# A decoder step's FFN on one core: the second token half's operands made early and kept in DRAM, products paired in PSUM banks

## The chip, the core and the metric

The kernel runs on one core of a Trainium2 chip. The time is device microseconds (us) of one launch; the figure to compare is the median of 3 runs. [...]

## The reference

One layer of a conditioned hybrid decoder over 1024 prompt tokens and 8 x 4 sample tokens (1056 in all), width 1024: a mixer (three kinds of recurrence), then the FFN that the change touches, then a last norm.

```
x = x + gate_m * concat(y_A, y_B, y_C) @ w_out
h = rms_norm(x, norm_ffn_w) * (1 + scale_f) + shift_f
g, u = split(h @ w_ffn_in)            # 1024 -> 2 x 2816
x = x + gate_f * ((silu(g) * u) @ w_ffn_out)
y = rms_norm(x, final_norm_w)
```

## The kernel before

The program is recorded, not written in order: every operation goes through `Plan.record`, and `Plan.order` lists them engine by engine with a cost table, the lowest key first among those that are ready (the key is the place of recording, less what `priority(n)` gives); tiles come from pools of numbered buffers (`tile(..., bufs)`), and `give` hands buffers of one tag to another once the first tag is done. So all rows of a profile bear one line, L632 (L639 after the change), and work is told apart by the tiles' names.

Values are kept as two fp32r parts, high and low, and one product is three matmuls (`dmm`: hi x hi, hi x lo, lo x hi). Splitting a tile is a cast on ACT (the high part) and a subtraction on DVE or POOL (the low part): `wh`, `wl` for weights, `act` pairs for the FFN's input, `raw` pairs for its inner values.

The tokens are cut into four pieces of 264 (`HW`), and the FFN runs twice (`g` = 0, 1), each time over two pieces, with all weights loaded again. In one `g`:

- `ffn_input` makes 7 operands (blocks) of 4 x 264 columns from x1: the normed pieces b11, b21, b12, b22 and their differences, as one two-by-two block product with seven products instead of eight needs them. Each block has a high and a low `act` tile; 14 of the 16 `act` tiles are in use.
- for each of 22 `f`, `ffn_up` loads four weight tiles of 256 KB (a11, a12: gate; a21, a22: up), forms s1 to s4 from them, splits seven weights, runs seven products of 12 matmuls each (84), adds them up on DVE in `sl` tiles, applies Silu on ACT, multiplies, and splits the result into `raw` pairs.
- after every second `f`, `down` loads four tiles of w_ffn_out and runs 16 groups of 6 matmuls (96), whose results DVE adds to x1 (`kp` tiles, `gated_half`). The last piece holds the 32 sample tokens, whose gates differ (`gated_seq`, a small `ga` tile).

A period below is this round of two `f` and one `down`: 168 + 96 = 264 matmuls. Weights are loaded into `wr` (4 buffers, plus the given ones: one of `tq`, one of `s0`, two of `int`), and split into four `wh`/`wl` pairs. At the end of `g` = 0, `ffn_input(..., 1)` uses again the `act` tiles that `g` = 0 read; at `g` = 1, `f` = 2, `final(x1, 0)` normalizes and writes the first 384 tokens in one go.

Of the kernel before, what the change touches and what calls it, by code (L numbers as in the profile page):

```python
# [13 lines left out]
F32 = mybir.dt.float32  # L14
# [52 lines left out]
ENGW = "ppvpvpvpvvv"  # L67
LEVELS = (1, 2, 4, 8, 16, 32)
# [171 lines left out]
class Plan:  # L240
# [17 lines left out]
    def tile(self, pool, shape, dt, tag, bufs=1, like=None):  # L258
# [8 lines left out]
        return View(t, ap.bitcast(dt) if ap.dtype != dt else ap, ())  # L267

# [380 lines left out]
class Step:  # L649
# [866 lines left out]
    def dmm(self, o, terms, first=True, last=True):  # L1516

        n = len(terms)
        for i, ((wh, wl), (xh, xl)) in enumerate(terms):
            self.nc.tensor.matmul(o, wh, xh, start=first and i == 0, stop=False)  # L1520
            self.nc.tensor.matmul(o, wh, xl, start=False, stop=False)
            self.nc.tensor.matmul(o, wl, xh, start=False, stop=last and i == n - 1)
# [171 lines left out]
    def ffn_input(self, x1, rs, sc, g):  # L1694
# [5 lines left out]

        def h(k, hf, i):
            t = self.raw()[:, 0:HW]
            x = x1[k]
            for si, o, d, n in self.half(hf, T):
                en(XR[4 * g + i]).tensor_tensor(t[:, d:d + n], x[si][:, o:o + n], rs[hf][:, d:d + n], op=ALU.mult)
            n = min(HW, TP - HW * hf)
            sh = self.mod[:, 3 * KT + k]
            if TSE[4 * g + i] == "s":
                nc.scalar.activation(t[:, 0:n], t[:, 0:n], AF.Identity, scale=sc[:, k, 0:1], bias=sh[:, 0:1])
            else:  # L1710
                nc.vector.tensor_scalar(t[:, 0:n], t[:, 0:n], sc[:, k, 0:1], sh[:, 0:1], op0=ALU.mult, op1=ALU.add)
            if n < HW:
                tv = t[:, n:HW].rearrange("p (q i) -> p q i", i=TQ)
                nc.vector.tensor_tensor(tv, tv, sc[:, k, 1:9].unsqueeze(2).broadcast_to([P, NQ, TQ]), op=ALU.mult)
                nc.vector.tensor_tensor(tv, tv, sh[:, 1:9].unsqueeze(2).broadcast_to([P, NQ, TQ]), op=ALU.add)
            return t

        def put(i, j, t):
            self.split(blk[i][0][:, j], blk[i][1][:, j], t, en(LOE[7 * g + i]))

        en = lambda c: nc.gpsimd if c == "p" else nc.vector
        b11 = []
        b21 = []
        for j in range(KH):
            b11.append(h(j, 2 * g, 0))
            put(0, j, b11[j])
# [471 lines left out]
```

## Time and profile before

| what | value |
|---|---|
| three runs | 1806.72, 1808.59, 1818.21 us; median 1808.59 |
| the profiled execution | 1816.74 us, its span 1814.9 us |
| busy | PE 94%, DVE 78%, ACT 53%, POOL 52% |
| mean granted TensorE clock | 0.958 |
| chain that ended last, by engine | PE 76%, DVE 10%, ACT 7% |

PE's busy share says that it nearly always has a matmul in flight, not that it works at its peak: a matmul that waits in the pipe, or runs at the lower clock level, counts as busy. So the argument goes by matmuls in a stretch of time, stage by stage. The mixer ends at about 920 us of the span; the output projection, the two FFN halves and the last norm fill the rest.

### The profile page before, as it was taken

Reading aid. Unit: us, or ns where it says so; the run is one execution under the profiler, and the core shown is the slowest. Engines: PE = TensorE matmul, PEld = TensorE weight load, DVE = VectorE, ACT = ScalarE, POOL = GpSimd, SP = SyncE. Lnnn points to the kernel's source line nnn. Section 1 sums busy time; section 2 is a strip of 40 time slices with the busy share of each in tenths; the row PEclk is TensorE's granted clock in tenths of the full one; section 3 lists DMA queues with packets and bytes.
Section 4 is the critical chain, followed back from the end, with each engine's and each line's share of the span. In section 5 each row is a group of like instructions: output and inputs, shape, how many; then the busy total and the mean of one; then the engine's idle time right before and its main releaser. Section 6 shows DMA issues by size and latency. Waiting matters only on the chain.

```text
span 1814.9 us, 43501 instructions
## 1 busy us (share of the span) xinstructions
PE 1710.4 (94%) x16278; PEld 1492.6 (82%) x16278; DVE 1407.0 (78%) x3426; ACT 964.9 (53%) x2406; POOL 946.8 (52%) x1068
## 2 busy tenths in 40 slices
PE   5999999999999999999899999999997889999995
PEld 2787776777788877777699999999996889999995
DVE  6664575777766667667758889899999989999997
ACT  5654555746666556768736555434445534434434
POOL 5552332533455535565527665666667546646645
PEclk9999898999999988999799999999997999999997
DMA  8313113123342211113342232332321232323321
GB/s 286 110 50 108 35 52 105 46 60 109 74 132 51 68 32 40 35 48 110 107 136 81 73 100 81 102 102 94 110 83 60 76 105 94 107 80 94 105 82 67
DMA packets 152923, 158.28 MB, mean 87 GB/s; under 512 B 67620, under 2 KB 94472, under 8 KB 152712
## 3 DMA queue, kind: packets, MB, share of 16 engines
q1 hardware_dynamic: 152136, 154.92, 28.3%
q8 instruction: 128, 2.10, 0.5%
q14 instruction: 83, 0.68, 0.1%
q10 hardware_dynamic: 576, 0.59, 0.1%
HBM read 142.55 MB, written 12.89 MB: 86 GB/s over the span
## 4 chain that ended last, share of the span: by engine, by line
PE 76%; DVE 10%; ACT 7%; issue 3%; DMA 2%; POOL 1%; SPq 0%; DVEq 0%; ACTq 0%; POOLq 0%
PE psd L632 29%; PE psc L632 15%; PE psg L632 14%; PE psm L632 10%; PE psi L632 8%; DVE kp L632 3%; DVE sl L632 2%; ACT sl L632 2%; ACT wh L632 2%; DVE act L632 1%; DVE wl L632 1%; DMA wr<-in_w_ada_dram 1%; ACT s L632 1%; DVE raw L632 1%; ACT ts L632 1%
## 5 line engine op out<-in xcount | busy, mean ns | idle before, releaser
L632 PE MATMUL psd<-act,wh 128*128 128x384 f32 (+3 forms) x2144 | 543.7, 331 | 18.7 <-ACT act L632 11.8
L632 POOL TENSOR_TENSOR wl<-wr,wh 128x512 fp32r<-128x512 f32 (+1 forms) x215 | 302.7, 1411 | 265.2 <-ACT wh L632 240.7
L632 PEld LDWEIGHTS psd<-act,wh 128*128 128x128 f32 x2144 | 372.1, 194 | 44.8 <-ACT act L632 15.2
L632 PE MATMUL psd<-act,wl 128*128 128x384 f32 (+3 forms) x1048 | 344.0, 328 | 2.6 <-POOL wl L632 1.6
L632 ACT CAST wh<-wr 128x512 fp32r<-128x512 f32 (+1 forms) x277 | 169.9, 618 | 194.3 <-PE psd L632 45.7
L632 ACT ACTIVATE sl<-sl 128x384 f32<-128x384 f32 (+5 forms) x400 | 187.7, 483 | 59.9 <-DVE sl L632 44.4
L632 PEld LDWEIGHTS psd<-act,wl 128*128 128x128 f32 x1048 | 203.3, 194 | 14.3 <-issue 3.7
L632 PE MATMUL psc<-act,wh 128*128 128x264 f32 (+2 forms) x776 | 157.4, 291 | 6.0 <-ACT act L632 3.9
L632 PE MATMUL psg<-act,wh 128*128 128x264 f32 (+1 forms) x784 | 157.8, 291 | 2.2 <-DVE act L632 1.1
L632 POOL TENSOR_TENSOR sl<-sl,sl 128x384 fp32r<-128x384 f32 (+5 forms) x84 | 83.9, 1000 | 102.5 <-ACT sl L632 39.9
L632 PEld LDWEIGHTS psc<-act,wh 128*128 128x128 f32 x776 | 123.2, 190 | 9.4 <-ACT act L632 5.1
L632 PEld LDWEIGHTS psg<-act,wh 128*128 128x128 f32 x784 | 124.9, 191 | 6.7 <-issue 2.0
L632 PE MATMUL psg<-act,wl 128*128 128x264 f32 (+1 forms) x392 | 113.9, 291 | 2.8 <-POOL wl L632 2.2
L632 PE MATMUL psc<-act,wl 128*128 128x264 f32 (+2 forms) x388 | 112.7, 290 | 1.5 <-POOL wl L632 1.1
L632 ACT COPY ts<-psg 64x128 f32<-64x128 f32 (+1 forms) x272 | 75.9, 279 | 63.8 <-PE psc L632 44.7
L632 POOL TENSOR_TENSOR wl<-int,wh 128x512 fp32r<-128x512 f32 (+1 forms) x61 | 85.7, 1407 | 41.5 <-ACT wh L632 38.3
L632 DVE TENSOR_TENSOR sl<-sl,sl 128x264 f32<-128x264 f32 (+2 forms) x136 | 93.9, 699 | 8.3 <-ACT sl L632 7.4
L632 POOL TENSOR_TENSOR wl<-tq,wh 128x512 fp32r<-128x512 f32 x42 | 59.2, 1410 | 61.5 <-ACT wh L632 61.1
L632 DVE TENSOR_TENSOR xb<-xb,qb 96x30 f32<-96x30 f32 (+3 forms) x270 | 85.0, 315 | 3.1
L632 ACT CAST wh<-int 128x512 fp32r<-128x512 f32 (+1 forms) x108 | 66.5, 615 | 37.0 <-PE psc L632 6.5
L632 ACT CAST raw<-sl 128x264 fp32r<-128x264 f32 x88 | 36.2, 411 | 91.1 <-DVE sl L632 20.5
L632 DVE TENSOR_TENSOR qb<-nb,xb 96x30 f32<-96x30 f32 (+3 forms) x270 | 76.3, 282 | 10.2 <-DMA xb<-in_masks_dram 6.3
(332 smaller groups left out, 4683.6 us busy)
## 6 DMA issues: line engine op xcount, KB each, us to landing
wr<-in_w_fi_dram SPq DMA_DIRECT2D x94, 256.0 KB
wr<-in_w_ada_dram SPq DMA_DIRECT2D x80, 256.0 KB
wr<-in_w_in_dram SPq DMA_DIRECT2D x62, 256.0 KB
wr<-in_w_fo_dram SPq DMA_DIRECT2D x49, 256.0 KB
int<-in_w_fi_dram SPq DMA_DIRECT2D x34, 256.0 KB
tq<-in_w_fi_dram SPq DMA_DIRECT2D x29, 256.0 KB
kp<-in_xT_dram SPq DMA_DIRECT2D x32, 192.0 KB
s<-in_w_fi_dram SPq DMA_DIRECT2D x19, 256.0 KB
```

Source lines behind the costliest of these rows:

```text
L632: getattr(getattr(nc, o.eng), o.fn)(*[real(a) for a in o.args], **{k: real(a) for k, a in o.kw.items()})
```

## The change

- The operands of `g` = 1 are made during `g` = 0: `ffn_stage` is a generator, started after `f` = 4, which makes one block column after another in new `hb` tiles (given by `int`, `ix` and `lora`), splits it into the two `act` tiles that were free, and writes it to DRAM (`xop`), 56 writes of 132 KB. It is advanced twice after each `f`. At `g` = 1, `ffn_back` fetches the seven blocks in 14 transfers of 528 KB.
- `int` buffers no longer go to `wr`.
- In `ffn_up` the products come in another order (x0, x3, x5, x2, x1, x4, x6); the first and the fifth, and the third and the seventh, are summed in one bank by PE; Silu, the products of gate and up, and the difference are written back in place in PSUM. DVE does five additions per `f`, not seven. Weight splits and sums are recorded with `priority(WPR)`, WPR = 100.
- `gated_seq` works in place in the bank, without `ga`.
- `final(x1, 0)` is advanced by one step per `f`.

```diff
@@ Step
+    def ffn_parts(self, x1, rs, sc, g, j, b11, b21, put, alloc):
...
+        b12 = h(j, 2 * g + 1, 2)
+        b22 = h(KH + j, 2 * g + 1, 3)
+        t1 = (self.hb if g else self.sl)()[:, 0:HW]
+        en(TAD[4 * g + 0]).tensor_tensor(t1, b12, b11, op=ALU.subtract)
+        t2 = (self.hb if g else self.sl)()[:, 0:HW]
+        en(TAD[4 * g + 1]).tensor_tensor(t2, b22, t1, op=ALU.subtract)
+        put(2, j, t2)
+        yield
...
+    def ffn_stage(self, x1, rs, sc):
...
+        self.xop = [nc.tile("dr", [P, 2, KH, HW], F32, f"xop{i}") for i in range(7)]
+        stg = [self.act()[:, 0:KH * HW].rearrange("p (k n) -> p k n", n=HW) for i in (0, 1)]
...
+        def put(i, j, t):
+            c = next(turn)
+            hi, lo = (st[:, c] for st in stg)
+            self.split(hi, lo, t, en(LOE[7 + i]))
+            for v, a in enumerate((hi, lo)):
+                nc.sync.dma_start(self.xop[i][:, v, j], a.bitcast(F32))
...
+    def ffn_back(self):
+        blk = [None] * 7
+        for i in (0, 3, 5, 2, 1, 4, 6):
+            blk[i] = [self.act()[:, 0:KH * HW] for v in (0, 1)]
+            for v in (0, 1):
+                self.nc.sync.dma_start(blk[i][v].bitcast(F32), self.xop[i][:, v].rearrange("p k n -> p (k n)"))
...
@@ ffn_up
-        nc.scalar.copy(p1, prod(w1, x[0]))
-        acc(ga, p1, prod(w2, x[1]))
-        nc.scalar.activation(ga, ga, AF.Silu)
-        u2 = p1
-        acc(u2, p1, prod(w6, x[2]))
-        acc(u3, u2, prod(ws(s3), x[3]))
-        c21 = self.sl()[:, 0:HW]
-        acc(c21, u3, prod(ws(a22), x[4]), ALU.subtract)
-        p5 = prod(ws(s1), x[5])
-        acc(u3, u3, p5)
-        acc(u4, u2, p5)
+        pa = prod(w1, x[0])
+        nc.scalar.copy(u2, pa)
+        pc = prod(w3, x[3])
+        pb = prod(w4, x[5])
+        acc(u2, u2, prod(ws(s2), x[2]))
+        acc(u3, u2, pc)
+        nc.scalar.activation(ga, prod(ws(a12), x[1], pa), AF.Silu)
+        pe = prod(ws(a22), x[4])
+        acc(pe, u3, pe, ALU.subtract)
+        acc(u3, u3, pb)
         s4 = a12
         add(s4, a12, s2)
-        acc(gb, u4, prod(ws(s4), x[6]))
-        nc.scalar.activation(gb, gb, AF.Silu)
+        prod(ws(s4), x[6], pb)
+        acc(pb, u2, pb)
+        nc.scalar.activation(pb, pb, AF.Silu)
         out = []
-        for a, b in ((ga, c21), (gb, u3)):
+        for a, b in ((pe, ga), (pb, u3)):
             nc.vector.tensor_tensor(a, a, b, op=ALU.mult)
@@ gated_seq
-        t = self.small(TS, tag="ga", bufs=2)
+        t = ps[:, d:d + TS]
@@ tile_hybrid_step_kernel
+    nc.make("sb", "hb")
+    for tag, to, n in (("tq", "wr", KH * P), ("s0", "wr", KH * P), ("int", "hb", HW), ("ix", "hb", HW), ("lora", "hb", HW)):
...
         if g:
-            x = st.ffn_input(x1, rs, sc2, 1)
+            x = st.ffn_back()
...
+            if g == 0 and f == 4:
+                late = st.ffn_stage(x1, rs, sc2)
             if g == 1 and f == 2:
-                for _ in st.final(x1, 0, o_y):
-                    pass
+                late = st.final(x1, 0, o_y)
+            with nc.priority(-LATER):
+                next(late, None)
+                if not g:
+                    next(late, None)
```

How the instructions stand, at three places. All engines' rows are the same as before up to the output projection.

DVE, before, at the end of the first half: `raw` and `sl` are the normed pieces and their differences, `act` the operand parts, `wl` a weight's low part.

```order
L632 TENSOR_TENSOR raw_907_33547<-raw_907_33547,mod_89 128x32
L632 TENSOR_TENSOR sl_909_33585<-raw_906_33534,raw_887_32883 128x264
L632 TENSOR_TENSOR wl_107<-int_112,wh_102 128x512
L632 TENSOR_TENSOR sl_910_33598<-raw_907_33547,sl_909_33585 128x264
L632 TENSOR_TENSOR act_128<-sl_909_33585,act_127 128x264
L632 TENSOR_TENSOR act_122<-sl_910_33598,act_121 128x264
L632 TENSOR_TENSOR act_124<-raw_906_33534,act_123 128x264
L632 TENSOR_TENSOR act_126<-raw_901_33455,act_125 128x264
L632 TENSOR_TENSOR act_130<-raw_907_33547,act_129 128x264
```

The five subtractions into `act` stand in one run there, four such runs one behind another. DVE, after, inside the first half (`int` and `lora` are `hb` buffers, `act_133` and `act_134` the staging pair):

```order
L639 TENSOR_TENSOR psc_117<-sl_714_26961,psc_117 128x264
L639 TENSOR_TENSOR sl_714_26961<-sl_714_26961,psd_151 128x264
L639 TENSOR_TENSOR psc_117<-psc_117,sl_713_26916 128x264
L639 TENSOR_TENSOR act_133<-int_112,act_134 128x264
L639 TENSOR_TENSOR act_133<-int_113,act_134 128x264
L639 TENSOR_TENSOR wl_106<-wr_96,wh_103 128x512
L639 TENSOR_TENSOR psd_151<-sl_712_26779,psd_151 128x264
L639 TENSOR_TENSOR raw_717_27096<-psc_117,raw_716_27035 128x264
L639 TENSOR_TENSOR act_133<-lora_94,act_134 128x264
L639 TENSOR_TENSOR psd_151<-psd_151,sl_714_26961 128x264
L639 TENSOR_TENSOR wl_105<-wr_97,wh_100 128x512
L639 TENSOR_TENSOR raw_719_27160<-psd_151,raw_718_27149 128x264
```

The operands' subtractions now stand between the first half's own rows, and those own rows have a bank as output (`psc`, `psd`).

SP, before, at the end of the first half: four rows of its last w_ffn_out weights and the four of the second half's first `f` (`tq`, `int` and `s_0` are weight buffers):

```order
L632 DMA int_112<-in_w_fo_dram 128x512
L632 DMA int_113<-in_w_fo_dram 128x512
L632 DMA wr_97<-in_w_fo_dram 128x512
L632 DMA tq_198<-in_w_fo_dram 128x512
L632 DMA wr_98<-in_w_fi_dram 128x512
L632 DMA wr_99<-in_w_fi_dram 128x512
L632 DMA s_0_195<-in_w_fi_dram 128x512
L632 DMA wr_96<-in_w_fi_dram 128x512
```

Nothing stands between them. SP, after, at the same place: `xop` are the operands in DRAM, of which block 0 was fetched earlier into the staging pair; the four w_fi rows are a11, a12, a21, a22 of the second half's first `f`.

```order
L639 DMA tq_198<-in_w_fo_dram 128x512
L639 DMA act_121<-xop_0_209 128x1056
L639 DMA act_122<-xop_0_209 128x1056
L639 DMA wr_98<-in_w_fi_dram 128x512
L639 DMA act_123<-xop_0_212 128x1056
L639 DMA act_124<-xop_0_212 128x1056
L639 DMA wr_97<-in_w_fi_dram 128x512
L639 DMA act_127<-xop_0_214 128x1056
L639 DMA act_128<-xop_0_214 128x1056
L639 DMA wr_99<-in_w_fi_dram 128x512
L639 DMA s_0_195<-in_w_fi_dram 128x512
```

Of that `f`, a11 and a12 now stand behind four and five fetched blocks, and a21 and a22 behind all six.

PE, before, in the first `f` of the second half, third and later products:

```order
L632 MATMUL psd_151<-act_120,wh_102 128x264
L632 MATMUL psd_151<-act_119,wl_107 128x264
L632 MATMUL psd_150<-act_127,wh_102 128x264
L632 MATMUL psc_117<-act_123,wh_103 128x264
L632 MATMUL psg_152<-act_121,wh_101 128x264
L632 MATMUL psd_150<-act_128,wh_102 128x264
L632 MATMUL psd_150<-act_127,wl_107 128x264
```

Three products' rows alternate. PE, after, at the same place (`act_121` is block 1 with a12's parts, `act_123` block 4 with a22's, `act_125` block 5 with s1's):

```order
L639 MATMUL psm_111<-act_121,wh_102 128x264
L639 MATMUL psm_111<-act_122,wh_102 128x264
L639 MATMUL psm_111<-act_121,wl_105 128x264
L639 MATMUL psi_172<-act_123,wh_102 128x264
L639 MATMUL psi_172<-act_124,wh_102 128x264
L639 MATMUL psi_172<-act_123,wl_105 128x264
L639 MATMUL psg_153<-act_125,wh_100 128x264
L639 MATMUL psg_153<-act_126,wh_100 128x264
L639 MATMUL psi_172<-act_123,wh_102 128x264
```

After the products of a11 and a12, the third product in line is that of a22, then those of s1 and s3.

## Rows read from the trace of the kernel before

**Rows 1.** Windows by stage: busy us (instructions) of each engine, clock, DMA.

```profile
core 0: us, PE busy (x) PEld busy (x) DVE busy (x) ACT busy (x) POOL busy (x), PEclk, DMA share, GB/s
1117.27:1345.41 228.14, 227.85 (x1850) 225.86 (x1849) 205.99 (x407) 98.79 (x196) 139.88 (x99) 1.00 0.31 98
1494.62:1767.44 272.82, 266.82 (x2114) 259.73 (x2113) 248.95 (x594) 113.56 (x224) 156.40 (x112) 1.00 0.30 94
1366.96:1494.62 127.66, 106.39 (x712) 97.44 (x711) 116.00 (x252) 60.86 (x127) 74.79 (x65) 0.85 0.24 77
...
1767.44:1814.90 47.46, 29.00 (x190) 25.53 (x188) 34.50 (x80) 21.03 (x42) 24.02 (x21) 0.81 0.18 64
961.20:1117.27 156.07, 151.95 (x1186) 146.94 (x1187) 138.75 (x269) 90.00 (x203) 104.90 (x94) 1.00 0.27 85
```

**Rows 2.** Windows of 10 us around the start of the second half, same columns.

```profile
1360.00:1370.00 10.00, 10.00 (x84) 10.00 (x83) 8.34 (x16) 5.89 (x13) 8.53 (x8) 1.00 0.58 182
...
1380.00:1390.00 10.00, 6.25 (x20) 4.12 (x18) 8.53 (x15) 8.95 (x20) 10.00 (x14) 0.67 0.09 27
1390.00:1400.00 10.00, 5.65 (x17) 4.24 (x18) 9.49 (x21) 6.10 (x14) 7.84 (x10) 0.50 0.16 52
...
1460.00:1470.00 10.00, 7.12 (x34) 6.41 (x35) 6.46 (x20) 4.08 (x6) 4.69 (x3) 0.66 0.37 118
```

**Rows 3.** PE's waits from 1366.96 to 1494.62: total us, times, longest us.

```profile
PE psd L632 <- ACT act L632: 6.3, 5, 2.5
```

**Rows 4.** PE's timeline in the second half: start us, us, [idle before, releaser].

```profile
1599.87 0.40 PE L632 MATMUL psg<-act,wh 128*128 128x264 f32 x2
1600.57 0.39 PE L632 MATMUL psg<-act,wl 128*128 128x264 f32 x1 [0.29 <-POOL wl L632]
```

**Rows 5.** DVE's groups, 1494.62 to 1767.44: count, busy us, mean ns.

```profile
L632 DVE TENSOR_TENSOR wl<-int,wh 128x512 fp32r<-128x512 f32 x22 | 28.5, 1294 | 0.4
L632 DVE TENSOR_TENSOR sl<-sl,sl 128x264 f32<-128x264 f32 x32 | 25.8, 824 | 0.0
L632 DVE TENSOR_TENSOR kp<-kp,ga 128x32 f32<-128x32 f32 x64 | 20.6, 323 | 0.0
L632 DVE TENSOR_TENSOR raw<-sl,raw 128x264 fp32r<-128x264 f32 x32 | 19.2, 600 | 6.7 <-ACT raw L632 6.5
...
L632 DVE TENSOR_TENSOR sl<-sl,psc 128x264 f32<-128x264 f32 x28 | 11.9, 425 | 6.0 <-PE psc L632 5.7
...
L632 DVE TENSOR_TENSOR wr<-int,wr 128x512 f32<-128x512 f32 x9 | 6.1, 679 | 0.0
...
L632 DVE TENSOR_TENSOR ga<-psd,mod 128x32 f32<-128x32 f32 x32 | 5.7, 177 | 0.0
```

**Rows 6.** DVE's groups, 1117.27 to 1345.41, same columns.

```profile
L632 DVE TENSOR_TENSOR raw<-sl,raw 128x264 fp32r<-128x264 f32 x28 | 21.5, 769 | 2.7 <-ACT raw L632 2.7
L632 DVE TENSOR_TENSOR sl<-sl,sl 128x264 f32<-128x264 f32 x29 | 21.5, 740 | 4.2 <-ACT sl L632 3.4
```

**Rows 7.** DVE's groups, 1366.96 to 1470, same columns.

```profile
L632 DVE TENSOR_TENSOR act<-raw,act 128x264 fp32r<-128x264 f32 x18 | 10.4, 593 | 4.1 <-ACT act L632 4.0
...
L632 DVE TENSOR_TENSOR act<-sl,act 128x264 fp32r<-128x264 f32 x8 | 5.4, 684 | 0.5 <-ACT act L632 0.5
...
L632 DVE TENSOR_TENSOR raw<-raw,mod 128x32 f32<-128x32 f32 x8 | 3.2, 405 | 0.0
```

**Rows 8.** Windows: five us near the program's start, columns as Rows 1.

```profile
10.00:15.00 5.00, 2.61 (x6) 1.50 (x7) 1.02 (x5) 2.54 (x9) 0.97 (x1) 1.00 1.05 375
```

**Rows 9.** Timelines of SP, DVE and ACT in the first half: issues and first readings of two loads.

```profile
1196.49 0.33 SPq L632 DMA_DIRECT2D wr<-in_w_fi_dram  x1
...
1200.44 0.68 DVE L632 TENSOR_TENSOR wr<-tq,wr 128x512 f32<-128x512 f32 x1
...
1207.66 0.33 SPq L632 DMA_DIRECT2D wr<-in_w_fo_dram  x1
...
1215.21 0.62 ACT L632 CAST wh<-wr 128x512 fp32r<-128x512 f32 x1 [1.17 <-PE psi L632]
```

More of the change, by code (lines that the diff above doesn't have):

```diff
@@ L67 @@
 ENGW = "ppvpvpvpvvv"
+WPR = 100
+LATER = 0
 LEVELS = (1, 2, 4, 8, 16, 32)
@@ L267, in tile, with make @@
         return View(t, ap.bitcast(dt) if ap.dtype != dt else ap, ())
+    def make(self, pool, tag):
+        self.phys[tag] = []
+        self.space[tag] = pool
     def give(self, tag, to, cut):
@@ L1514, in wr, with dmm @@
         return self.nc.tile("sb", [P, KH, P], F32, "wr", 4)
-    def dmm(self, o, terms, first=True, last=True):
+    def dmm(self, o, terms, first=True, last=True, on=False):
         n = len(terms)
+        kw = {"skip_group_check": True} if on else {}
         for i, ((wh, wl), (xh, xl)) in enumerate(terms):
-            self.nc.tensor.matmul(o, wh, xh, start=first and i == 0, stop=False)
-            self.nc.tensor.matmul(o, wh, xl, start=False, stop=False)
-            self.nc.tensor.matmul(o, wl, xh, start=False, stop=last and i == n - 1)
+            self.nc.tensor.matmul(o, wh, xh, start=first and i == 0, stop=False, **kw)
+            self.nc.tensor.matmul(o, wh, xl, start=False, stop=False, **kw)
+            self.nc.tensor.matmul(o, wl, xh, start=False, stop=last and i == n - 1, **kw)
     def dense(self, w, xs, chunks, evac, banks=None, wt=None, warm=0):
@@ new lines, in put @@
+        def put(i, j, t):
+            self.split(blk[i][0][:, j], blk[i][1][:, j], t, en(LOE[i]))
+        bs = []
+        for i in (0, 1):
+            for j in range(KH):
+                k = KH * i + j
+                bs.append(self.ffn_h(self.raw()[:, 0:HW], x1[k], rs[0], sc, k, 0, en(XR[i]), TSE[i]))
+                put(i, j, bs[-1])
+        for j in range(KH):
+            for _ in self.ffn_parts(x1, rs, sc, 0, j, bs[j], bs[KH + j], put, self.raw):
+                pass
+        return blk
@@ L1771, in ffn_up @@
         w1 = ws(a11)
-        w2 = ws(a12)
         add(s1, a21, a22, ALU.add)
@@ L2033, with cut @@
             out_proj(m, h, wt, yb, 0)
+    nc.make("sb", "hb")
+    for tag, to, n in (("tq", "wr", KH * P), ("s0", "wr", KH * P), ("int", "hb", HW), ("ix", "hb", HW), ("lora", "hb", HW)):
+        def cut(ap):
+            ap = ap if len(ap.shape) == 2 else fl(ap)
+            parts = [ap[:, o:o + n] for o in range(0, ap.shape[1] - n + 1, n)]
+            return [x.rearrange("p (k n) -> p k n", n=P) for x in parts] if to == "wr" else parts
+        nc.give(tag, to, cut)
     for g in (0, 1):
         if g:
-            x = st.ffn_input(x1, rs, sc2, 1)
-        fin = []
+            x = st.ffn_back()
+        fin, late = [], iter(())
         def down(f0, gs):
@@ L2071 @@
         pass
-    for tag in ("tq", "s0", "int"):
-        nc.give(tag, "wr", lambda ap: [fl(ap)[:, o:o + KH * P].rearrange("p (k n) -> p k n", n=P)
-                                       for o in range(0, ap.shape[1] * ap.shape[2] - KH * P + 1, KH * P)])
     nc.order()
```

110 lines of the change are left out of this document (58 added, 52 removed).

## Prediction

> **What bounds the kernel now.** First the windows by stage [rows 1]: from 1117 us to the end PE is the engine to watch, so I count matmuls per stretch. Seven periods of the first half take 228.14 us, 32.6 us each, and 228.14 / 1848 = 123.5 ns per matmul. Eight periods of the second half take 272.82 us, 34.1 us each, for the same matmuls. Between the two lie 127.66 us with 708 matmuls (the last `down`, five `ffn_up`, two `down`): at 123.5 ns that is 87.4 us, so 40.2 us are lost there. DVE is the busiest of the helpers: 29.4 us of a first-half period, 31.1 us of a second-half one.
>
> [...] PE's largest wait there is for ACT's `act` tiles, the operands of the second half, 2.5 us at the longest [rows 3]. So the boundary is bound by making operands, on which the halved clock comes down as well (0.85 over the stretch, that is 0.15 x 127.66 = 19 of the 40 us).
>
> Third, why a second-half period is 1.5 us longer: PE's waits there are for low parts of weights, as the 0.29 us at 1600.57 [rows 4], which DVE and POOL make late. DVE has more to do there, above all the small `kp`/`ga` rows [rows 5].
>
> **The change part by part.**
>
> *Boundary.* The operand making leaves it. What is late next is the fetch: block 0 is already in the staging pair, the six others are 6 x 2 x 540,672 bytes = 6.49 MB, and a21 and a22, without which five of its first seven products can't start, stand behind them on SP. Let T be the start of the first half's last `f`. Its first block is released at T + 1.5 us (12 x 123.5 ns), so the first fetch flows at about T + 3.5 us, my allowance for issue and landing being 2 us (the shortest load of [rows 9] is read 4.0 us after its issue). Ahead of a21's end lie 6.49 MB, two w_ffn_out and two w_ffn_in tiles and a21 itself, 7.8 MB; at the 375 GB/s that the DMA engines reach when full [rows 8] that is 20.8 us, so a21 is there at T + 24.3. PE needs it after 84 + 96 matmuls of the first half (22.2 us) and the products of a11 and a12 (3.0 us): T + 25.2. From landing to the first matmul go a sum (DVE 0.68 to 1.29 [rows 5]), a cast (0.62 [rows 9]) and a low part (0.68 to 1.29), about 2.5 us: the third product starts near T + 26.8, 1.6 us late; and since the order gives s1, s2, s3 their `wh` buffers ahead of a12 and a22, those two pass through one buffer, a cast and a low part, 1.3 us, more each. I take 4.5 us of stall. Whether the clock falls can't be told: it fell after waits of this size [rows 2, 3], and the window at 1460 lost 0.34 of its clock, 3.4 us. I count half of that. Together 6 us of the 40.2 stay: **gain 34.2 us**. Bounds: nothing stays (40), or 20 stay (the stall plus three quarters of the 19 us that the clock costs now).
>
> [...]
>
> *DVE per period.* Two additions fewer per `f`: 4 x 0.425 = 1.7 us [rows 5]. Four multiplies, now of two SBUF tiles at 0.824 (0.740 in the first half [rows 6]), get an operand in PSUM; the nearest row with one is the addition from a bank, 0.425: 1.6 us (1.3). Four low parts of 0.600 (0.769), likewise: 0.7 us (1.4). In the second half eight `kp`/`ga` rows of 0.323 become rows with a bank, nearest 0.177: 1.2 us. Sum 5.2 us in the second half, 4.3 us in the first. Writing into a bank in place has no row; I take it at the price of reading one, and if it cost 0.2 us more for each of the 12 results per period, 2.4 us of the saving would go.
>
> [...]
>
> *Second half, steady.* DVE falls from 31.1 to 25.9 us per period, under the 29.4 us with which the first half runs at 32.6. I let the second half come to that pace: 8 x 1.5 = **12 us**. `final(x1, 0)`, now spread over the periods, adds to DVE what it took from the boundary, less than 1 us per period. Bounds 6 (half of it) and 19 (120 ns per matmul, the pace of the 1360 window).
>
> *First half.* It now carries the operands. On DVE: 28 low parts, 18 x 0.593 and 8 x 0.684 in the rows, together 17.4 us for 28; 16 rows on sample columns at 0.4, 6.4 us; 8 differences, about 4 us [rows 7]. In all 28 us over seven periods, 4.0 us each, against 4.3 us saved: even. But they come in four bursts, not evenly, and behind a burst wait the first half's own additions and low parts. SP takes 56 writes in its queue, each waiting for a low part on DVE, with the next weights behind it. And `wr` has six buffers where it had eight. Against that, loads run ahead: the `wr` issued at 1196.49 is first read at 1200.44, 4.0 us later, which is the shortest and comes once in a period; the next shortest is that of 1207.66, read at 1215.21, 7.5 us later [rows 9]; two buffers less cost 2 x 32.6 / 12 = 5.4 us of lead on average. Weights first helps, at no cost that I see while banks are free. I take **2 us lost**, bounds 4 gained and 12 lost.
>
> *Before 1117 and after 1767* [rows 1]. The early stretch has 1186 matmuls, 9.6 us over the pace; lighter DVE and fewer weight buffers pull both ways: nothing, plus or minus 3. The end gains **1 us** from lighter DVE, bounds 0 and 3.
>
> **Sum.** 34 + 12 - 2 + 0 + 1 = 45 us. The profiled execution took 1816.74 us, 8 us over the median of the three runs; 1816.7 - 45 = 1771.7, and from the median 1808.6 - 45 = **1764 us**.
>
> **The rivals**, from the median.
> 1. *The pace is better* (no stall at the boundary, 120 ns in both halves): 6 + 7 + 6 us more gained, 1745. For it: 84 matmuls in 10 us occur [rows 2]. Against: even the undisturbed first half doesn't hold it.
> 2. *The clock falls for long at the boundary*: 20 us stay, 1764 + 14 = 1778. For it: the fall now begins within 10 us of the first waits. Against: now DVE starves PE for 30 us, then one late weight.
> 3. *The first half pays*: DVE and POOL, slowed by each other (the same subtraction takes 0.68 or 1.29 us [rows 5]), let it sink to the second half's 34.1 us: 7 x 1.5 = 10.5 us instead of 2, 1773; at twice that, 1783. [...]
> 4. *The boundary keeps its loss*, the fetch taking the operands' place: if it ran at a third of the rate, 1764 + 34 = 1798, no change that can be told. Against: 375 GB/s.
> 5. *Weights starve* (slower): with six buffers the load that is now read 4.0 us after its issue comes too late in every `f`; a wait of 1.5 us x 44 = 66 us, 1830. It turns the sign from 45 / 44 = 1.0 us per `f` on. Against: eleven loads of twelve have 7.5 us or more to draw on [rows 9], and a load of 256 KB takes 0.7 us at the rate of [rows 8].
>
> **How the numbers follow.** Forecast 0.52, rival 1 0.12, 2 0.16, 3 0.11, 4 0.04, 5 0.05. The range reaches from rival 1 to the far end of rival 3 and past rival 2: 1744 to 1785; outside it lie rivals 4 and 5 and the edges of the others. About 1% (18 us) is what three runs with such a spread can tell from no change. Below 1790.5: 0.89; within 1%: 0.06; above: 0.05.
>
> **What would show it.** In the profile after: 708 matmuls around the boundary in some 93 us, no window of 10 us there with fewer than 40, and PE's wait there for a weight or a DMA, not for `act`; second-half periods of 32.6 us with DVE at 26 us; first-half periods within 0.5 us of 32.6. It is wrong if first-half periods exceed 34 us, if PE waits for weights in every `f`, or if the clock is at its lower level for over 15 us at the boundary.

## The result, and the profile after

The changed kernel takes **1784.23 us** (1782.81 to 1787.32, four runs) against 1810.09 us (1806.72 to 1818.21, four runs) of the kernel before beside it: ratio 0.9839 [0.9809, 0.9869], 26 us gained where 45 were forecast. The profiled execution took 1787.32 us, its span 1785.5, that is 29.4 less than before. Its first stretch, up to the 9,558th matmul of the trace (900.1 us in the kernel before), holds hardly anything of the change and was 6.3 us shorter; over all kernels of this study it took 888.9 to 903.4 us. So I compare stages, cut at the same matmul rows (each trace has 16,278), and not spans.

The windows by stage, at the same rows of PE and in the same order as [rows 1] (us; busy us and instructions of PE, its matmuls, PEld, its weight loads, DVE, ACT and POOL; granted clock, DMA share, GB/s):

```profile
1115.50:1356.02 240.52, 231.60 (x1851) 226.93 (x1849) 203.29 (x418) 108.36 (x224) 153.47 (x117) 1.00 0.39 120
1474.97:1741.77 266.80, 262.28 (x2114) 260.33 (x2113) 223.87 (x573) 119.62 (x234) 153.14 (x112) 0.99 0.33 102
1378.33:1474.97 96.64, 90.80 (x712) 87.53 (x711) 77.83 (x185) 39.51 (x82) 54.19 (x39) 1.00 0.41 143
1741.77:1785.50 43.73, 27.79 (x190) 24.93 (x188) 28.57 (x73) 20.36 (x42) 21.09 (x19) 0.78 0.22 76
954.83:1115.50 160.67, 152.38 (x1186) 148.17 (x1187) 133.42 (x268) 103.47 (x224) 117.19 (x108) 0.99 0.31 98
```

Against [rows 1]: boundary 127.66 to 96.64, 31.0 gained; second half 272.82 to 266.80, 6.0 gained; end 47.46 to 43.73, 3.7 gained; first half 228.14 to 240.52, **12.4 lost**; early stretch 156.07 to 160.67, **4.6 lost**. With 0.8 lost between first half and boundary that is 22.9 in what the change touches; the other 6.4 of the 29.4 came from the stretch ahead.

The boundary is what it was forecast to be. Its windows of 10 us, as in [rows 2]:

```profile
1380.00:1390.00 10.00, 9.60 (x74) 9.00 (x73) 7.87 (x24) 3.24 (x7) 3.87 (x3) 1.00 1.04 415
1390.00:1400.00 10.00, 7.35 (x52) 6.29 (x51) 3.58 (x8) 2.93 (x6) 4.26 (x4) 1.00 0.41 155
```

The worst window has 52 matmuls at a granted clock of 1.00, where there were 20 at 0.67 and 17 at 0.50; the fetch fills the DMA engines (share 1.04, 415 GB/s) and the clock stays up (1.00 in both windows). PE's longest waits there, as in [rows 3] (total us, times, longest us), are short and none is for `act`:

```profile
PE psi L639 <- DVE raw L639: 0.9, 1, 0.9
PE psm L639 <- ACT sl L639: 0.9, 1, 0.9
PE psd L639 <- POOL wl L639: 0.8, 1, 0.8
```

DVE's prices came out as taken from their nearest rows. Its groups in the second half, 1474.97 to 1741.77, answering to [rows 5]:

```profile
L639 DVE TENSOR_TENSOR psd<-psd,mod 128x32 f32<-128x32 f32 x32 | 6.3, 198 | 0.9
...
L639 DVE TENSOR_TENSOR kp<-kp,psc 128x32 f32<-128x32 f32 x33 | 5.9, 180 | 0.3
...
L639 DVE TENSOR_TENSOR psc<-sl,psc 128x264 f32<-128x264 f32 x8 | 3.5, 435 | 3.3 <-PE psc L639 3.3
L639 DVE TENSOR_TENSOR psc<-psc,sl 128x264 f32<-128x264 f32 x8 | 3.5, 433 | 0.3 <-ACT sl L639 0.3
```

Writing into a bank in place cost here what reading one did (0.43 against 0.425 taken), and the small rows cost 0.18 and 0.20 (0.177 taken). Still, DVE's busy time fell to 28.0 us of a second-half period (223.87 / 8), not to 25.9.

The loss is in the periods that make the staged operands. Windows of the periods one by one, the five long ones of the first half and the one long period of the second:

```profile
1079.13:1115.50 36.37, 33.80 (x258) 32.84 (x257) 33.47 (x63) 23.10 (x44) 26.88 (x24) 0.95 0.41 125
1115.50:1151.16 35.66, 33.08 (x266) 32.43 (x265) 33.62 (x66) 18.72 (x39) 25.82 (x23) 1.00 0.44 133
1151.16:1187.12 35.96, 34.22 (x266) 32.69 (x265) 33.48 (x66) 17.34 (x38) 25.34 (x21) 1.00 0.42 130
1187.12:1222.91 35.79, 33.30 (x266) 32.45 (x265) 32.78 (x71) 16.18 (x35) 22.97 (x18) 1.00 0.50 156
1222.91:1257.22 34.31, 33.18 (x266) 32.42 (x265) 26.28 (x55) 14.08 (x29) 20.94 (x16) 1.00 0.39 119
1539.68:1579.20 39.52, 35.42 (x266) 34.10 (x265) 30.06 (x76) 20.15 (x36) 19.38 (x14) 0.96 0.34 101
```

In four of them DVE is busy for 33 of 36 us. The first reading is therefore that DVE is full. Over the whole first half DVE has no more work than before, so its total can't be the reason. The windows from the 10,987th to the 13,091st matmul row, eight periods, of the kernel before,

```profile
1084.11:1345.41 261.30, 260.74 (x2106) 257.59 (x2105) 237.04 (x468) 116.24 (x229) 159.72 (x113) 1.00 0.31 98
```

and of the changed kernel:

```profile
1079.13:1356.02 276.89, 265.40 (x2107) 259.76 (x2105) 236.75 (x480) 131.45 (x268) 180.35 (x140) 0.99 0.39 120
```

DVE has the same work to 0.3 us, as the prediction had it ("even"); what grew is ACT's busy time by 15 us and POOL's by 21, and the time by 15.6.

### The profile page after: what moved, and what is told of

Read it like the earlier page. It is cut to its first block, busy times and chain, and to the rows that moved or that the text cites. A ratio compares the mean times of both kernels' runs of the same rounds, so it can differ in the third digit from the quotient of the medians.

```text
span 1785.5 us, 43412 instructions
## 1 busy us (share of the span) xinstructions
PE 1689.8 (95%) x16278; PEld 1481.9 (83%) x16278; DVE 1324.8 (74%) x3338; ACT 969.4 (54%) x2412; POOL 941.3 (53%) x1068
## 5 line engine op out<-in xcount | busy, mean ns | idle before, releaser
L639 PE MATMUL psd<-act,wh 128*128 128x384 f32 (+3 forms) x2152 | 535.3, 327 | 11.7 <-ACT act L639 4.9
L639 PEld LDWEIGHTS psd<-act,wh 128*128 128x128 f32 x2152 | 369.0, 193 | 35.4 <-ACT act L639 7.2
L639 ACT CAST wh<-wr 128x512 fp32r<-128x512 f32 x351 | 213.7, 617 | 209.9 <-PE psd L639 50.3
L639 ACT ACTIVATE sl<-sl 128x384 f32<-128x384 f32 (+6 forms) x312 | 150.8, 500 | 18.7 <-POOL sl L639 6.7
L639 PE MATMUL psc<-act,wh 128*128 128x264 f32 (+1 forms) x752 | 148.8, 289 | 3.3 <-ACT wh L639 3.3
L639 DVE TENSOR_TENSOR wl<-wr,wh 128x512 fp32r<-128x512 f32 x127 | 124.7, 990 | 20.8 <-ACT wh L639 19.4
L639 PE MATMUL psc<-act,wl 128*128 128x264 f32 (+1 forms) x376 | 107.4, 287 | 0.5 <-DVE wl L639 0.5
L639 POOL TENSOR_TENSOR wl<-s,wh 128x512 fp32r<-128x512 f32 x45 | 62.8, 1395 | 65.4 <-ACT wh L639 57.4
L639 PE MATMUL psm<-act,wh 128*128 128x264 f32 (+1 forms) x400 | 78.6, 288 | 1.5 <-ACT sl L639 0.9
L639 PEld LDWEIGHTS psg<-act,wl 128*128 128x128 f32 x392 | 73.8, 189 | 3.1 <-POOL wl L639 2.3
L639 PE MATMUL psi<-act,wh 128*128 128x264 f32 x376 | 72.3, 286 | 2.1 <-ACT wh L639 2.1
```

Of the source, the lines that this page charges most:

```text
L639: getattr(getattr(nc, o.eng), o.fn)(*[real(a) for a in o.args], **{k: real(a) for k, a in o.kw.items()})
```

## The experiments

The theory at the start: the staged operands crowd DVE in five periods. Its rivals: the writes at the head of SP's queue hold up weights; the loss is the new products' or the missing two `wr` buffers'; DVE and POOL slow each other. Below are the eight periods of each half and the boundary between them, each cut at the same matmul rows; this boundary begins 96 rows later than that of [rows 1]:

| kernel | median us | ratio to before | first half, 8 periods | boundary | second half, 8 periods |
|---|---|---|---|---|---|
| before | 1810.09 | 1 | 261.30 | 115.39 | 272.82 |
| after | 1784.23 | 0.9839 [0.9809, 0.9869] | 276.89 | 83.75 | 266.80 |
| six buffers | 1811.68 | 1.0 [0.9973, 1.0027] | 258.42 | 113.6 | 275.12 |
| products only | 1797.9 | 0.9911 [0.9883, 0.994] | 263.36 | 112.87 | 260.06 |
| no staging | 1764.39 | 0.9729 [0.9688, 0.9771] | 260.87 | 78.17 | 263.42 |
| write only | 1770.56 | 0.9769 [0.9738, 0.9801] | 261.61 | 83.56 | 263.5 |
| make only | 1777.29 | 0.9805 [0.9769, 0.9842] | 272.04 | 78.18 | 263.5 |
| writes on ACT | 1793.98 | 0.9892 [0.9874, 0.9911] | 285.58 | 84.0 | 267.4 |
| low parts on POOL | 1784.7 | 0.9844 [0.9817, 0.9872] | 270.43 | 83.0 | 265.5 |
| paced | 1799.04 | 0.9922 [0.9902, 0.9942] | 282.11 | 83.7 | 263.7 |
| low priority | 1789.04 | 0.9873 [0.9844, 0.9903] | 276.40 | 83.7 | 265.1 |
| no Ln, Exp | 1782.07 | 0.9832 [0.9784, 0.988] | 276.8 | 83.7 | 260.88 |
| Ln, Exp together | 1784.34 | 0.9849 [0.9822, 0.9875] | 279.07 | 84.5 | 261.73 |
| joined | 1769.01 | 0.9784 [0.9746, 0.9822] | 266.46 | 83.63 | 260.38 |

Where stages and medians differ by some us, I go by the stages: up to the 9,558th row alone "low parts on POOL" took 903.4 us and "after" 893.8, with nothing in it that the edit touches. The stages have their noise too. In "after", "low priority" and the two kernels on Ln and Exp, the rows of PE, DVE, ACT and POOL in the first half's eight periods stand in the same order, and these took 276.40 to 279.07 us: a difference under 3 us there tells nothing.

**No staging.** Leaves out the operands of the second half: it multiplies with those of the first.

```diff
-            x = st.ffn_back()
+            pass
...
-            if g == 0 and f == 4:
-                late = st.ffn_stage(x1, rs, sc2)
```

> The changed kernel without the making, the writing and the fetching of the second half's operands: the second half multiplies with the first half's operands again, so its values are left out. Theory A (the first half pays because the operand work is crammed on DVE into five of its periods, or by the writes that come with it): first-half periods fall from 35.8 to 32.5 us, 16 to 18 us less there, and the boundary loses its 8 us: about 1758 us. Theory B (six weight buffers where there were eight, or the new order in ffn_up, make the first half slower): first-half periods stay at 34 us or more, and the time falls by the boundary alone, to 1774 us or so.

```profile
1085.52:1346.39 260.87, 259.12 (x2106) 257.44 (x2105) 205.25 (x431) 115.75 (x228) 154.13 (x112) 1.00 0.28 97
1380.43:1458.60 78.17, 76.56 (x616) 75.39 (x615) 64.23 (x155) 36.02 (x74) 46.46 (x33) 1.00 0.28 95
```

The first half is as before in sum, with DVE at 205 us where it was 237: lighter DVE gives nothing back there. That DVE wasn't the limit fits the kernel before, where PE is busy for 227.85 of 228.14 us [rows 1]. The sum hides that the periods alternate: 32.25 us from 1182.60 to 1214.85 and 33.49 from 1214.85 to 1248.34, for instance, where the seven of [rows 1] take 32.5 to 32.7 each. Why every second one is longer with the new products is open. The staging costs 276.89 - 260.87 = 16.0 us here, and the fetch 83.75 - 78.17 = 5.6 at the boundary. The staged work on DVE is 236.75 - 205.25 = 31.5 us.

**Six buffers.** The kernel before, without the two buffers that `int` gave.

```diff
-    for tag in ("tq", "s0", "int"):
+    for tag in ("tq", "s0"):
```

> The kernel before with one edit: the two int buffers are not given to the weights, so six weight buffers instead of eight, as after the change. If weight buffers are what the first half lacks after the change, periods here go from 32.6 to 34 us or more and the time rises by 20 us or more; if not, it stays within 3 us of the kernel before.

```profile
1083.87:1342.29 258.42, 257.71 (x2106) 256.85 (x2105) 235.98 (x467) 117.06 (x229) 156.37 (x112) 1.00 0.29 98
```

2.9 us less in the one half, 2.3 more in the other (275.12 against 272.82): nothing in sum. Rival 5 is out.

**Products only.** The kernel before with the new `dmm`, `ffn_up`, `gated_seq` and `WPR`; operands made at the boundary as before.

```diff
-    def dmm(self, o, terms, first=True, last=True):
+    def dmm(self, o, terms, first=True, last=True, on=False):
...
+            with nc.priority(WPR):
+                self.split(hi, lo, t, next(eng))
...
+            o = self.bank()[:, 0:HW] if ps is None else ps
```

> The kernel before with the new product order, the paired banks, the results in PSUM and the weights first, without the operands made early (eight weight buffers, operands made at the boundary). If the lighter DVE is worth what I said, second-half periods fall from 34.1 to 32.4 us and first-half ones stay at 32.5: 13 us less in the second half, and a little at the boundary, about 1794 us. The rival: without the rest it brings nothing, since the periods wait for weights, and the time stays at 1809.

```profile
1079.39:1342.75 263.36, 260.16 (x2107) 257.59 (x2105) 217.32 (x431) 113.72 (x228) 151.23 (x111) 1.00 0.28 96
...
1490.87:1750.93 260.06, 260.06 (x2114) 258.91 (x2113) 221.70 (x561) 110.28 (x225) 149.76 (x112) 1.00 0.29 98
```

This is where the second half's gain is from: 12.8 us, 32.5 per period, with DVE at 27.7 us per period and not 25.9. Lighter DVE, the new order and weights first are all in this kernel, so which of them gives the gain isn't shown. The first half took 2 us more, so the new products don't explain 16.

**Writes on ACT.** The 56 writes leave SP's queue.

```diff
-                nc.sync.dma_start(self.xop[i][:, v, j], a.bitcast(F32))
+                nc.scalar.dma_start(self.xop[i][:, v, j], a.bitcast(F32))
```

> The changed kernel with the 56 staging writes issued from ScalarE's queue in place of SP's, so that no weight load stands behind a write that waits for a low part. Five first-half periods of the changed kernel took 36.4, 35.7, 36.0, 35.8 and 34.3 us where the kernel before took 32.6. If the writes at the head of SP's queue make the weights late (SP waited 23 us for operand tiles in 107 us), those periods fall to 33 to 34 us and the median of 1784 to about 1774. If the crowding of VectorE does it (94% busy there), they stay within 0.5 us of 36 and the median at 1784 plus or minus 4; ScalarE's own waits for the low parts could even add a few us.

The first half went up to 285.58. SP is free of the writes, and it is worse. I read it so that a wait for a low part that stood ahead of a load now stands ahead of casts of weights, but no row shows such a wait by itself. The clock is part of it: 0.97 over the eight periods, against 0.99 in the changed kernel. That doesn't clear SP, since the wait was moved, not removed.

**Low parts on POOL.**

```diff
-LOE = "vvvvvvvvvvvvvv"
+LOE = "vvvvvvvppppppp"
```

> The changed kernel with the 28 low parts of the staged operands on GpSimd in place of VectorE. By the theory of a crowded VectorE, 28 x 0.8 = 22 us leave it, GpSimd takes some 28 x 0.95 = 27 us in its place (it is busy for 26 of 36 us there), the five periods fall to about 34 us and the median to about 1776. If it is not VectorE's own time but the slowing of VectorE and GpSimd by each other (0.68 against 1.29 us for the same subtraction), the periods stay at 36 us or grow, and the median is 1784 to 1790. If SP's queue decides, the writes come later with GpSimd and the median is over 1784 too.

The first half fell to 270.43, 6.5 us less, although POOL's work rose from 180 to 201 us beside DVE. So more work on POOL beside DVE didn't cost time: that each is slower beside the other (DVE's 264 columns 0.90 us on average in place of 0.42, last section) can't be what decides alone, and POOL is not the limit. The median stayed at 1784.7, where 1776 was expected; in the profiled run the start was 9.6 us longer.

**Paced.** Each step of the staging may not be planned ahead of the first product of its `f`.

```diff
+            here = next(o for o in nc.ops[n0:] if o.eng == "tensor")
...
+                for _ in range(steps(f) - steps(f - 1)):
+                    next(late, None)
+                for o in nc.ops[n1:]:
+                    nc.after(here, o)
```

> The changed kernel with the steps of the staging held back in the planner: each may not start before the first product of the f that it is recorded in, seven steps to four f from f = 4 to 19, so that the order has them over eight periods and not crammed into five. The computation is the same. By the theory that crowding costs more than in proportion, VectorE is at about 30.5 of 32.5 us in eight periods and the first half's loss of 18 us falls to between 5 and 10: 1772 to 1777. If each staged operation costs its time wherever it stands (VectorE as the bound of the first half, crowded or not), the loss stays and is only spread, 34.5 us for each of eight periods: 1784. If writes in SP's queue decide, the same, 1784, since as many writes stand there.

```profile
1258.61:1298.06 39.45, 34.87 (x267) 33.97 (x265) 29.54 (x64) 16.36 (x34) 23.61 (x20) 0.96 0.39 121
1298.06:1333.41 35.35, 34.03 (x266) 32.57 (x265) 28.08 (x60) 15.56 (x34) 22.94 (x18) 1.00 0.34 100
```

My theory falls here. With DVE at 28.1 us in a period, less than the 29.4 of the kernel before [rows 1], the second of these still takes 35.4 us, and there are more of them: 282.11 in all. Against the same rows of "no staging" seven of the eight periods are 0.7 to 3.6 us longer, and the first one shown 7.1: there PE waited 2.6 us for a low part on POOL, and the granted clock was 0.96 over the period. Not DVE's fullness, but staged work standing in a period at all costs some 2.7 us of each on average. A stall of that kind in the timeline of this kernel (start us, us, and in brackets the idle time before and who ended it):

```profile
1314.50 2.38 POOL L639 TENSOR_TENSOR int<-kp,gb 128x264 f32<-128x264 f32 x2
...
1315.74 0.58 ACT L639 ACTIVATE int<-int,mod,sc 128x232 f32<-128x232 f32 x1 [1.35 <-POOL int L639]
...
1317.04 1.53 POOL L639 TENSOR_TENSOR wl<-s,wh 128x512 fp32r<-128x512 f32 x1 [0.17 <-ACT wh L639]
...
1317.35 1.27 DVE L639 TENSOR_TENSOR int<-int,sc 128x32 f32<-128x32 f32 x1
...
1318.86 1.51 POOL L639 TENSOR_TENSOR wr<-tq,wr 128x512 f32<-128x512 f32 x1 [0.28 <-DVE int L639]
...
1320.40 0.62 ACT L639 CAST wh<-wr 128x512 fp32r<-128x512 f32 x1 [2.23 <-POOL wr L639]
...
1321.08 0.50 PE L639 MATMUL psg<-act,wh 128*128 128x264 f32 x2 [0.60 <-ACT wh L639]
```

Read from the end: PE waits for a weight's cast, ACT had waited 2.23 us for a sum of weights on POOL, and POOL had first made two staged products (2.38 us) and then a weight's low part (1.53 us). Before the sum it stood 0.28 us more, by the trace for DVE's staged `int` of 32 columns, which took 1.27 us. ACT earlier waited 1.35 us for POOL's staged `int`, with casts behind it. In these rows staged work stands on POOL (2.38 us), ACT (0.58) and DVE (1.27) ahead of work for weights; one staged operand passes through POOL, ACT, DVE, ACT, DVE. This is one stall; that the others are like it isn't shown.

**Make only** and **write only.** The first computes the staged operands, but leaves out the writes and the fetch (the second half multiplies with the first half's operands):

```diff
-            for v, a in enumerate((hi, lo)):
-                nc.sync.dma_start(self.xop[i][:, v, j], a.bitcast(F32))
...
-            x = st.ffn_back()
+            pass
```

The second leaves out the making, and writes and fetches as much (the first half's operands):

```diff
+            for v in (0, 1):
+                nc.sync.dma_start(self.xop[i][:, v, j], x[i][v][:, j].bitcast(F32))
```

> The changed kernel with the staged operands computed as before, but neither written to DRAM nor fetched back: 56 writes and 14 fetches are left out, and the second half multiplies with the first half's operands. Without staging altogether the first half from 1050 us on had periods of 31.3 to 33.5 us, with it 34.3 to 36.4 in five of them. If making the operands is what costs (VectorE, GpSimd and ScalarE each take staged work in their queues ahead of weights), the five periods stay at 35 to 36 us, and only the boundary gains some 5 us: 1779. If the writes in SP's queue are what costs, the five periods fall to 33 us and the time to about 1767.

> The changed kernel with 56 writes of the same size and the same 14 fetches, but nothing staged is computed: the writes take the first half's operands, which are there already, four writes an f from f = 4 to 17, and the second half multiplies with those. If making the operands is what costs, the first half is as without staging (periods of 32.3 and 33.5 us), and the boundary keeps the 35.6 us that the fetch gives it: about 1769. If the writes cost by themselves (issue time on SP, traffic), the periods stay at 35 to 36 us: 1782.

Make only:

```profile
1086.52:1358.56 272.04, 262.92 (x2107) 258.06 (x2105) 234.50 (x481) 130.42 (x268) 181.88 (x140) 1.00 0.27 93
```

Write only:

```profile
1081.70:1343.31 261.61, 259.70 (x2106) 257.52 (x2105) 205.20 (x431) 115.86 (x228) 154.05 (x112) 1.00 0.38 127
```

Over "no staging", making alone costs 11.2 us of the first half, writing alone 0.7, which is within the noise, both together 16.0: some 4 us come only with both. I read them as writes that wait for what is being made: in the five staged periods of the changed kernel SP waited 31.7 us for staged tiles. The clock has a part in these 4, by my estimate 1.8 us (0.05 x 36.37): in the first long period of the changed kernel the granted clock was 0.95, over the stretch of "make only" 1.00. The fetch alone gives the boundary of the changed kernel (83.56 against 83.75 us).

**Low priority.** `LATER` 600 in place of 0.

```diff
-LATER = 0
+LATER = 600
```

> The changed kernel with the staging steps (and those of final(x1, 0)) 600 places later in the planner's order of preference, so that each engine takes a staged operation only where the planner sees nothing else ready. If staged operations hurt by standing ahead of weight operations that are ready at that moment, the first half loses 5 to 10 us less: 1774 to 1779. If the planner gave them idle time already, and the loss comes from the chip running otherwise than the planner thinks, the periods stay at 35 to 36 us and the median at 1784 plus or minus 4.

276.40 against 276.89: nothing, and nothing could come of it. In these eight periods the rows of PE, DVE, ACT and POOL stand in the same order as in the changed kernel, tile for tile by name, so 600 places changed no choice there. What staged work behind the weights would cost this run doesn't show.

**No Ln, Exp** and **Ln, Exp together.** The one long period of the second half, 39.52 us, has `final(x1, 0)` in it. ACT's timeline there in the changed kernel:

```profile
1550.30 1.28 ACT L639 ACT_TABLE_LOAD   x1
1551.59 0.62 ACT L639 ACTIVATE s<-s,eps 128x384 f32<-128x384 f32 x1
...
1553.26 1.28 ACT L639 ACT_TABLE_LOAD   x1
...
1555.52 1.28 ACT L639 ACT_TABLE_LOAD   x1
1556.82 0.53 ACT L639 ACTIVATE s<-s 128x384 f32<-128x384 f32 x1
...
1561.82 1.28 ACT L639 ACT_TABLE_LOAD   x1
```

A Silu (1554.56) has come between Ln (1551.59) and Exp (1556.82), and four table loads of 1.28 us stand there, 5.1 us; in the kernel before, where no Silu stood between the two, it was two, at 1447.19 and 1463.51 us. The first kernel leaves the inverse root of `final(x1, 0)` out (the outputs are scaled by the mean square):

```diff
-            self.rsqrt(r, r, 0, nc.scalar.copy(r, ps))
+            nc.scalar.copy(r, ps)
```

> The changed kernel without the Ln and the Exp of the first 384 tokens' last norm (its factor is left as the mean square, so those values are left out). Two of ACT's table loads per function go with them. If the one slow period of the second half (39.5 us, where its neighbours take 32.4) comes from ACT changing tables between Silu and this norm, it falls to 33 us or so and the time by 6 us, to 1778. If it comes from the norm's products on PE or from DVE's additions, it stays at 38 us or more.

The second keeps it, and holds earlier Silus ahead of the copy and later ones behind Exp:

```diff
+            cp = nc.scalar.copy(r, ps)
+            self.gate = self.rsqrt(r, r, 0, cp)
+            for o in self.silus:
+                nc.after(o, nc.ops[n0])
...
+        if self.gate is not None:
+            self.nc.after(self.gate, o)
```

> The changed kernel with the second half's Silus held so that Ln and Exp of final(x1, 0) stand together in ScalarE's order: two table loads of 1.28 us there in place of four. The period that took 39.52 us fell to 32.85 without Ln and Exp. If the table loads are the cost, the period falls to about 35 us and the median by 3 to 5, to 1780. If it is the chain from Ln to the scaled outputs that makes PE wait, the period stays at 38 to 40 us and the median at 1784.

Its two periods there:

```profile
1550.87:1583.48 32.61, 32.61 (x267) 32.34 (x265) 25.25 (x70) 16.51 (x33) 18.71 (x14) 1.00 0.33 103
1583.48:1617.10 33.62, 33.17 (x266) 32.49 (x265) 32.07 (x80) 15.30 (x30) 19.17 (x14) 1.00 0.43 137
```

The long period is gone either way, and the second half takes 260.88 and 261.73 us. So it hangs on the four loads, not on the chain from Ln to the outputs. But they aren't the whole of its 7.1 us over the pace of 32.4. In "no staging", "make only" and "write only" the same four loads stand in this period, and it takes 36.0 us, here in "no staging":

```profile
1523.36:1559.39 36.03, 34.09 (x267) 32.69 (x265) 28.09 (x74) 20.17 (x36) 19.76 (x14) 1.00 0.33 110
```

That is 3.6 us over the pace. The other 3.5 us of the changed kernel stand behind the loads:

```profile
1569.24 1.29 POOL L639 TENSOR_TENSOR wr<-wr,tq 128x512 f32<-128x512 f32 x1 [2.02 <-DMA tq<-in_w_fi_dram]
...
1570.57 1.76 DVE L639 TENSOR_TENSOR wr<-wr,wr 128x512 f32<-128x512 f32 x1 [0.99 <-POOL wr L639]
...
1573.44 0.51 PE L639 MATMUL psd<-raw,wh 128*128 128x264 f32 x2 [2.05 <-DVE kp L639]
```

A sum on POOL waits for a load, DVE for that sum, PE 2.05 us for the additions behind DVE's own sum; the granted clock from 1571 to 1580 us was 0.81. Why the load came late is open. Both medians stay at about that of the changed kernel; in the profiled runs the gain of 5 to 6 us stands against a start up to the 9,558th row that took 7 to 8 us longer than that of "after".

**Joined.** Low parts on POOL, Ln and Exp together, and each pair of writes held in the planner until the next staged low part is made:

```diff
+            for w in prev:
+                nc.after(nc.ops[-1], w)
+            prev[:] = [nc.sync.dma_start(self.xop[i][:, v, j], a.bitcast(F32)) for v, a in enumerate((hi, lo))]
```

> The changed kernel with three edits: the staged low parts on GpSimd, Ln and Exp of final(x1, 0) held together, and each pair of staging writes held in the planner until the next staged low part is made, so that it finds its data ready when it reaches the head of SP's queue. By the parts run alone, in the profile: staged low parts on GpSimd took the eight periods from 1084 to 1345 us (of the kernel before) from 276.9 to 270.4 us, the held Ln and Exp the second half's eight from 266.8 to 261.7, and writes that wait cost 276.9 - 272.0 = 4.9 us. If the parts add up, the two stretches take 266 and 262 us and the median is about 1784 - 16 = 1768. If the moved low parts and the moved writes act on the same waits, the first stretch stays at 270 and the median is about 1773. If the later writes hold staging slots so long that the operands bunch up further, it is 1778 or more.

```profile
1077.22:1343.68 266.46, 263.37 (x2106) 258.25 (x2105) 224.92 (x454) 131.72 (x268) 201.80 (x166) 1.00 0.39 126
...
1461.87:1722.25 260.38, 259.93 (x2115) 258.66 (x2113) 221.06 (x573) 117.57 (x232) 152.02 (x112) 1.00 0.31 104
```

Both stretches came out at the sum of the parts or under it, 266 and 260 us, and the median at **1769.01 us** (1765.3 to 1778.55, six runs), the fastest that computes everything. The held writes took 4.0 us off "low parts on POOL" in the first half, a little over the noise; the clock is 1.00 there and was 0.99. SP's waits in the five staged periods (total us, times, longest us), "low parts on POOL" first,

```profile
SPq L639 <- ACT act L639: 34.2, 21, 3.6
...
SPq L639 <- POOL act L639: 12.9, 17, 1.6
```

then "joined":

```profile
SPq L639 <- POOL act L639: 6.1, 6, 2.8
...
SPq L639 <- ACT act L639: 5.8, 3, 3.2
```

47 us of waiting for staged operands at the head of SP's queue became 12. How long SP waits isn't the price, though: in the changed kernel it is 31.7 us (19.0 for ACT, 12.7 for DVE), less than the 47, and its first half is 6.5 us longer.

## Why the prediction was right, and where it was off

The time fell into the range, 20 us over the forecast, because one term was mis-sized by 11 us, three others by 3 to 6; the boundary, more than half of the forecast gain, held. That it fell inside is in part luck: 1784.23 is 0.8 us from the edge, and two of the four runs (1785.10 and 1787.32) are past it. By the prediction's own signs it was wrong in the first half: five periods there took 34.3 to 36.4 us, over the 34 that it names.

- **Boundary, 34.2 forecast, 31.0 measured.** Right in mechanism and nearly in size. With the fetch left out the stage takes 78.17 us, with it 83.75: the fetch costs 5.6 us (6.7 by the rows of [rows 1], 89.92 and 96.64), against the 6 that were to stay. The half chance of a low clock that the 6 contain didn't come (clock 1.00), so the stall was a little longer than the 4.5 taken. The other 2.5 us (89.92 against the 87.4 of the pace) are lost whether there is a fetch or not.
- **Second half, 12 forecast, 6.0 measured.** The pace is right: periods of 32.35 us, and 12.8 us with the products alone, though DVE saved 3.4 us of a period there (31.1 to 27.7) and not 5.2. What the sum lacked is the one period of 39.52 us: four table loads, 3.6 us, and a late weight behind them with the clock that it cost, 3.5. I had priced the spread `final(x1, 0)` by DVE alone ("less than 1 us per period") and not its Ln and Exp on ACT, which in the kernel before fell into the boundary (with table loads of 2 x 1.28 us).
- **First half, "I take 2 us lost".** This is the step that failed: 12.4 us lost, just past the bound of 12, and 0.8 more behind it. Its sum was right, 31.5 us of making on DVE (28 taken) against 31.8 saved (237.04 - 205.25), so that DVE's work stayed equal to 0.3 us; the inference from an equal sum to an equal time was wrong. Savings on DVE were worth nothing in the first half, as the kernel without staging shows. Making alone costs 11.2 us ("make only"), and staged work costs as much where DVE has room ("paced"). I had also left the staged work on ACT and POOL out of the sum, 16 and 26 us (131.45 - 115.75 and 180.35 - 154.13). The caveat on SP's queue ("each waiting for a low part") was right, for some 4 us.
- **Early stretch, 0 plus or minus 3 forecast, 4.6 lost.** The first staged period lies in it. It has the same cause: without staging the rows from 961 to 1117 us of the kernel before take 155.5 us (961.3 to 1116.8).
- **End, 1 forecast, 3.7 gained**, with "products only" as much (43.6 us from its second half's end to the end of its span): undersized. It comes with the products; that lighter DVE is the reason is argued.
- **Rival 3**, the first half paying, was what came to pass: its farther price, 1783 us, is the measured time to 1 us. That match is luck: it takes 21 us lost in the first half where 12.4 were, and the other terms made up the rest. Its reason, DVE and POOL slowed by each other, agrees with the trace of the changed kernel (512 columns on DVE 0.68 us with POOL idle and 1.31 beside it, last section), but isn't shown to be the cause, since more work on POOL made it faster (276.89 to 270.43 us). Rival 1 is out by the stall at the boundary, rival 2 by the clock of 1.00 there, rivals 4 and 5 by the 415 GB/s of the fetch and by six buffers, which cost nothing.
- **Operands in PSUM**, taken at 0.425 us, were priced rightly: operations on banks came at 0.43 us for 264 columns, as the row had it, and between SBUF tiles the same took 0.42 to 0.43 us in the changed kernel where POOL was idle. What the prediction took for the price of SBUF, 0.60 to 0.82 us, are means over operations with POOL idle (0.42 to 0.44 us) and with POOL beside them (up to 1.31, last section).

**Still open:** why a period with 3.5 staged steps ("paced") loses about as much as one with 5.6, and so what the first half's 11 us of making are made of. The timeline shows one chain of it, and no run took POOL's or ACT's part of the making away by itself, or put staged work behind the weights. What is left to "joined" over "no staging" in the first half is 266.46 - 260.87 = 5.6 us.

## What to carry to other kernels

Equal busy time is not equal time (DVE's 237.04 and 236.75 us stood in 261.30 and 276.89 us): work that is moved into a stage costs by the queues that it enters, so count its instructions on every engine that it passes through, and ask what stands behind each of its waits. A saving counts only in the stage whose limit it is: the new products took 3.4 us of DVE per period off one half and gained 1.6 us there, and 4.0 off the other ("no staging") and gained nothing. When moved work brings a different ACT function with it, hold its calls together (four table loads of 1.28 us and what stood behind them made a period of 32.4 us one of 39.52); and let a transfer enter a shared queue only when its data is ready (the held writes took 4.0 us off the first half, a little over the noise).

## What the runs showed of the hardware

- A small DVE operation on SBUF tiles beside a busy POOL was mostly dearer than its size tells: 264 columns took 0.90 us on average, and 0.42 with POOL idle. In the crowded stretch of the changed kernel, DVE's groups from 1115.5 to 1223 us:

```profile
L639 DVE TENSOR_TENSOR act<-int,act 128x264 fp32r<-128x264 f32 x14 | 10.9, 784 | 0.0
...
L639 DVE TENSOR_TENSOR act<-ix,act 128x264 fp32r<-128x264 f32 x3 | 3.1, 1019 | 0.0
...
L639 DVE TENSOR_TENSOR ix<-ix,sc 128x32 f32<-128x32 f32 x3 | 2.2, 724 | 0.0
```

The low parts that took 0.593 and 0.684 at the boundary [rows 7] take 0.784 and 1.019, and three rows of 32 columns between SBUF tiles take 0.724 us on average, where nine others there take 0.18 and 32 columns in a bank 0.198. That this goes with POOL's work shows when the changed kernel's `TENSOR_TENSOR` instructions on DVE from 1079.13 to 1356.02 us are sorted by what POOL did meanwhile. Of those with 264 columns, 6 between SBUF tiles with POOL idle took 0.42 to 0.43 us; 17 with POOL busy for at least 90% of their time took 0.42 to 1.41, 0.90 on average. With a bank among the inputs all 142 took 0.41 to 0.44, of which 87 had POOL busy beside them. In the second half of the kernel before, 24 between SBUF tiles with POOL idle took 0.42 to 0.44 us, and 8 with POOL busy for at least 90% of their time 1.29 to 1.31. So with one bank as an input DVE's time didn't change with POOL's work. With 512 columns, all between SBUF tiles, 40 on DVE with POOL idle took 0.67 to 0.69 us, and 32 with POOL busy for at least 90% of their time 0.72 to 1.79, 1.31 on average; on POOL 3 with DVE idle took 1.26 to 1.29, and 64 with DVE busy for at least 90% of their time 1.27 to 1.76, 1.46 on average (changed kernel, the same stretch).

- The DMA engines moved 415 GB/s in 10 us of the fetch, over the 375 that I had taken for full from [rows 8].
- Up to the 9,558th matmul row the profiled runs differ by 14.5 us (888.9 to 903.4) with almost the same program, more than most effects here; medians of four to six runs hide effects of 5 us that stages cut at the same row show, to within some 3 us in the first half's eight periods.
